# An encoder block on one core: where the values take their tokens' scale, and when late sums and late weights are prepared

## The chip, the cores and the metric

One Trainium2 chip, one of its cores. The metric is the time of one execution in microseconds (us) on the device. TensorE (PE in the profile) multiplies matrices into PSUM; VectorE (DVE), ScalarE (ACT) and GpSimd (POOL) work on whole tiles of 128 partitions; SyncE (SP) starts transfers. Each engine takes its instructions strictly in the order in which they were written for it.

## The reference, cut to what matters

One layer of a hybrid encoder on 256 tokens of width 2048. The mixing half (attention heads and Fourier groups) is left out here. The change lies in the feed-forward half:

```python
h  = rmsnorm(x, norm2_g)                      # per token: x * rstd * g
up = h @ w_up;  gate, val = up[:, :5504], up[:, 5504:]
gate = conv3_over_tokens(gate, dw_w) + dw_b   # depthwise, three neighbouring tokens
act  = gelu(gate) * val
x    = x + act @ w_down
y    = rmsnorm(x, normf_g)
```

The token scale `rstd` of the first norm is one number per token. It must be in the gates before the convolution, which mixes neighbouring tokens, and before the GELU. The value enters as a plain factor of its token's row of `act`, so its scale may be applied anywhere up to the addition to `x`.

## The kernel before

All matmuls are made of three: each operand is split into a high part (a rounded copy, made on ACT) and a low part (the rest, made on DVE as `raw - hi`), and high times high, low times high and high times low are summed in PSUM. So every weight tile of 128x2048 must be loaded (SP), copied (ACT, line 182 or 942) and subtracted (DVE, line 183 or 943) before TensorE can use it. The split tiles (`parts`) have three buffers, the loaded tiles (`raw`) three, and the tiles of the down-projection (`rawd`) two. `PLACES` says at which offset within its buffer a split tile starts: `"moving"` (0, 0), `"thirds"` (0, 32), `"product"` (28, 28) columns for the two parts.

The feed-forward half is a list of items (`ff_items`), one after the other on TensorE: a `gate` or `val` item makes 128 columns of the up-projection for all tokens, transposed (48 matmuls, line 351, or line 338 and 340 for the first ones); a `product` item is one of seven products (`P1`, `P2`, `N3`, `N4`, `N5`, `P6`, `P7`) by which a set of the down-projection over two blocks of tokens and two halves of columns is done with seven block products in place of eight (12 matmuls, lines 1050 to 1052). The sets are (group g, columns c); the last ones are (4, 0) and (4, 1). Four `down` items (24 matmuls each, lines 321 to 323, written as `ps_l`, from `w_down_late`) and four `last` ones (from `w_down_last`, lines 1197 to 1199, written as `ps_e`) do the last seven tiles of the hidden width without the seven products. The order of the items is written out by hand in `PATTERNS`; the end of it is val, down 0, P6, down 1, P2, down 2, N4, down 3 and then the `last` products.

What goes along with item n is set by `ff_step(n)`, called behind the matmuls of item n. It first runs the list `beside[n]`, then splits the weights for item n + 2 (`split_item`, which also starts further loads), then runs the list `behind[n]`. `at(list, n, f, ...)` enters work in these lists. So the place in a list is the place in the queues of ACT and DVE, in front of or after a split that TensorE will need two items later.

- `scaled_sum` (lines 832 to 842) takes a gate or a value out of PSUM at item n + 1 and multiplies it by `r2b`, the tokens' scale spread over all partitions, on DVE. For early items, which leave two sums in PSUM, ACT copies one of them first. `gate_conv`, `gate_gelu` and `val_mult` follow at n + 2.
- `product_out` (1016) adds P2, N3 and N4 to `x` and collects P6 and P7 in `Z`, `down_out` (1054) adds the `down` items' sums to `x`, `last_post` (1072) those of the `last` ones, all on DVE.
- `shared_out` (1029) runs once for each c, at its last set: P1, N5, P6 and P7, which were held over all sets, are combined and added to `x`, in three steps of two, three and three DVE instructions. The steps run behind items n + 2, n + 3 and n + 4, where n is the item P6.
- The weights of `last` 0 to 2 are split as those of other items. `split_last(3)` splits those of `last` 3 into two `rawd` tiles. It is written ahead of `last_product(0, 0)`, the first of the products of `last`. `last_product(c, b)` multiplies by the weights c for the token block b, and then runs `last_post` (addition on DVE, sum of squares on ACT) and `gain` (POOL). The first call also runs the `ff_step` that splits the weights of `last` 2. Then come the final norm's scale (`most_of`, `last_scale`) and `finish`, once for each token block.

Of the kernel before, what the change touches and what calls it, by code (L numbers as in the profile page):

```python
# [9 lines left out]
F32R = mybir.dt.float32r  # L10
AF = mybir.ActivationFunctionType
ALU = mybir.AluOpType

P = 128
D = 2048
S = 256
# [40 lines left out]
LAST = list(range(40, NF))  # L57
# [36 lines left out]
def block_kernel(  # L94
# [18 lines left out]
    nc = tc.nc  # L113
# [14 lines left out]
    units = [(w_in[i], 2048, "first" if i < N_QK else "still") for i in range(24)]  # L128
# [4 lines left out]
    for n, it in enumerate(items):  # L133
        if it[0] == "product":
            continue
        up_index[n] = len(units)
        if it[0] in ("gate", "val"):
            form = "still" if n < FIRST_PRODUCT else "thirds"
            units.append((w_up[2 * it[1] + (it[0] == "val")], 2048, form))
        elif it[0] == "down":  # L140
            units.append((w_down_late[4 * it[1] + it[2]], 2048, "moving"))
        else:
            units.append((w_down_last[it[1]], 512 * len(LAST), "moving"))
    RAW = 3
    raws, halves = {}, {}


    PLACES = {"still": (0, 16), "thirds": (0, 32), "first": (16, 16), "moving": (0, 0), "product": (28, 28)}
# [55 lines left out]
    xs = [base.tile([P, 2, 512], F32, tag=f"xs{c}", name=f"xs{c}") for c in range(4)]  # L204
# [60 lines left out]
    ps = bank(dn, "ps_warm")  # L265
# [13 lines left out]
    def rstd_of(ssq, width, name, n=2, r=None):  # L279

        var = base.tile([P, n], F32, tag="var" + name, name="var" + name)
        nc.vector.tensor_scalar(var, ssq, 1.0 / width, EPS, ALU.mult, ALU.add)
        if r is None:
            r = base.tile([P, n], F32, tag="rstd" + name, name="rstd" + name)
        nc.gpsimd.tensor_tensor(r, var, half_pow[:, 0:n], ALU.pow)
        return r
# [23 lines left out]
    def spread(r, dst, name):  # L310

        nc.vector.tensor_copy(dst, spread_sums(spread_diagonals(r, name), name)[:, :S])
# [76 lines left out]
    for c in range(4):  # L389
        t = base.tile([P, 4, 512], F32R, tag=f"hT{c}", name=f"hT{c}")  # L390
        hT.append(t)
    ps_u = [bank(mm, f"ps_u{b}") for b in range(2)]
    for k in range(NK):
        c, q = k // 4, k % 4
# [4 lines left out]
        hi, lo = halves[c]  # L399
# [392 lines left out]
    for n, (c, kq) in enumerate(OUT_ORDER):  # L792
        i = N_OUT + n
# [14 lines left out]
        if kq >= 2:  # L808
            part = "a" if kq == 2 else "f"
            ps = ps_a[c] if kq < 3 else ps_a[c, "f"]  # L810
# [15 lines left out]
    fp = ctx.enter_context(tc.tile_pool(name="fp", bufs=2))  # L826
# [3 lines left out]
    gate_out, sums_of, act = {}, {}, {}  # L830

    def scaled_sum(ps, name, whole):
        add = fp.tile([P, S], F32, tag="fadd", name=f"fa_{name}", bufs=3)
        if whole:
            nc.vector.tensor_tensor(add, ps[:, 0:S], r2b, ALU.mult)
            sums_of[name] = add
            return
        tmp = fp.tile([P, 512], F32, tag="ftmp", name=f"ft_{name}", bufs=1)[:, 0:S]
        nc.scalar.activation(tmp, ps[:, S : 2 * S], AF.Copy)
        nc.vector.tensor_tensor(add, ps[:, 0:S], tmp, ALU.add)  # L840
        nc.vector.tensor_tensor(add, add, r2b, ALU.mult)
        sums_of[name] = add

    def gate_conv(j):
        ga = sums_of.pop(f"g{j}")
# [170 lines left out]
    def product_out(g, c, p, ps):  # L1016
        tt = nc.vector.tensor_tensor
        if p in ("P6", "P7"):
            z = Z[c, p]
            if g == 0:  # L1020
                nc.scalar.activation(z, ps, AF.Copy)
            else:
                tt(z, ps, z, ALU.add)
        else:
            n, t = {"P2": (0, 0), "N3": (1, 0), "N4": (0, 1)}[p]
            xb = xs[2 * n + c][:, t, :]
            tt(xb, ps, xb, ALU.add)

    def shared_out(c):
        p1, n5, u, p7 = held[c, "P1"], held[c, "N5"], Z[c, "P6"], Z[c, "P7"]  # L1030
        x00, x10, x01, x11 = (xs[2 * n + c][:, t, :] for n in range(2) for t in range(2))
        w = wp.tile([P, 512], F32, tag="junk", name=f"sum01_{c}")
        tt = nc.vector.tensor_tensor
        tt(u, p1, u, ALU.add)
        tt(x00, p1, x00, ALU.add)
        yield
        tt(w, n5, u, ALU.subtract)
        tt(u, u, p7, ALU.add)
        tt(x01, x01, w, ALU.add)
        yield  # L1040
        tt(w, w, p7, ALU.subtract)
        tt(x10, x10, u, ALU.add)
        tt(x11, x11, w, ALU.add)

    def by_parts(ps, o, hi, lo, first, last, tiles, step, at):

# [6 lines left out]

    def down_out(c, pss):
        for b in range(2):
            xb = xs[c][:, b, :]
            nc.vector.tensor_tensor(xb, pss[b], xb, ALU.add)

    ssq3 = base.tile([P, 2, 5], F32, tag="ssq3", name="ssq3")

# [10 lines left out]

    def last_post(c, b, ps, o=0, n=512, part=None):

        xb = xs[c][:, b, o : o + n]
        nc.vector.tensor_tensor(xb, ps, xb, ALU.add)
        square_sum(c, b, c if part is None else part, o, n)

    def most_of(b, n):
# [42 lines left out]
        still_weights(hi, lo, ps, range(12, NK))  # L1121
    tot2 = base.tile([P, 2], F32, tag="tot2", name="tot2")
    nc.vector.tensor_reduce(tot2, ssq2, mybir.AxisListType.X, ALU.add)
    spread(rstd_of(tot2, D, "2"), r2b, "2")
    ff_step(1)
    up_posts(1, *items[0], pair[0][0])
    up_posts(2, *items[1], pair[1][0])
# [1 line left out]
    for n, it in enumerate(items):  # L1129
        if n < 2:  # L1130
            continue
        if it[0] == "last":
            break
        if n in (FIRST_PRODUCT - 9, FIRST_PRODUCT - 8):
            ring_load()
        if n == FIRST_PRODUCT - 6:
            pending.append(lambda: first_sums(*SETS[0]))
        if it[0] in ("gate", "val"):
            kind, j = it
            ps = bank(mm, f"ps_{kind}{j}")  # L1140
            if n < FIRST_PRODUCT:
                still_weights(*halves.pop(up_index[n]), ps, range(NK), lag=4 if n == 2 else 0)
            else:
                still_thirds(*halves.pop(up_index[n]), ps)
            ff_step(n)
            up_posts(n, kind, j, ps)
            continue
        if it[0] == "product":
            kind, g, c, p = it
            hi, lo = halves.pop(it)  # L1150
            both = c == 2
            shape = (2, 1024) if both else (4, 512)
            for cc in (0, 1) if both else (c,):
                o = 512 * cc if both else 0
                if (cc, p) in held:
                    first, end = (g, c) == FIRST_SET[cc], (g, c) == LAST_SET[cc]
                    by_parts(held[cc, p], parts[p], hi, lo, first, end, *shape, o)
                    continue
                ps = bank(mm, f"ps_{p}{g}{cc}")
                by_parts(ps, parts[p], hi, lo, True, True, *shape, o)  # L1160
                at(beside, n + 1, product_out, g, cc, p, ps)
            if (g, c) == LAST_SET.get(c) and p == "P6":
                todo = shared_out(c)
                for m in range(2, 5):
                    at(behind, n + m, next, todo, None)
        else:
            kind, g, c = it
            hi, lo = halves.pop(up_index[n])
            ps = [bank(mm, f"ps_l{g}{c}{b}") for b in range(2)]
            for b in range(2):  # L1170
                moving_weights(hi, lo, 512, LATE, act.get, b, ps[b], True, True)
            at(beside, n + 1, down_out, c, ps)
            if (g, c) == (0, 0):
                gfb = base.tile([P, D], F32, tag="hT0", name="gfb")
                nc.gpsimd.dma_start(gfb, normf_g.partition_broadcast(P))
        ff_step(n)
# [4 lines left out]

    def split_last(c):
        raw, n = raws[i + c], 512 * len(LAST)
        hi = fp.tile([P, 2048], F32R, tag="rawd", name=f"hi{i + c}")
        lo = fp.tile([P, 2048], F32R, tag="rawd", name=f"lo{i + c}")
        halves[i + c] = (hi, lo)
        nc.scalar.activation(hi[:, 0:n], raw[:, 0:n], AF.Copy)
        nc.vector.tensor_tensor(lo[:, 0:n], raw[:, 0:n], f32(hi[:, 0:n]), ALU.subtract)

    def last_product(c, b, o=0, n=512, part=None):  # L1190
        hi, lo = halves[i + c]
        ps = bank(dn, f"ps_e{c}{b}{o}")[:, 0:n]
        for q, k in enumerate(LAST):
            w = slice(q * 512 + o, q * 512 + o + n)
            ah, al = (act[k][:, p * S + b * P : p * S + (b + 1) * P] for p in range(2))
            end = q == len(LAST) - 1
            nc.tensor.matmul(ps, ah, hi[:, w], start=q == 0, stop=False)
            nc.tensor.matmul(ps, al, hi[:, w], start=False, stop=False)
            nc.tensor.matmul(ps, ah, lo[:, w], start=False, stop=end)
        if (c, b) == (0, 0):  # L1200
            ff_step(items.index(("last", 0)))
        last_post(c, b, ps, o, n, part)
        if c < 3:
            gain(c, b)

    split_last(3)
    for c in range(4):
        last_product(c, 0)
    r3 = last_scale(0, 3, most_of(0, 3))
    last_product(0, 1)  # L1210
# [115 lines left out]
```

## Time and profile before

| what | value |
|---|---|
| runs | 958.85, 958.19, 958.24 us, median 958.24 |
| profiled execution | 958.71 us, its span 956.9 us |
| busy, share of the span | PE 98%, DVE 76%, ACT 55%, POOL 5% |
| mean granted TensorE clock | 0.994 |
| HBM read, over the span | 211.80 MB, 224 GB/s |

The span runs from the first to the last instruction of the profiled execution. The 1.8 us between it and that execution's time lie outside of what the profile shows. Times inside the trace are counted from the start of the span.

### The profile page before, as it was taken

Reading aid. Unit: us, or ns where it says so; the run is one execution under the profiler, and the core shown is the slowest. Engines: PE = TensorE matmul, PEld = TensorE weight load, DVE = VectorE, ACT = ScalarE, POOL = GpSimd, SP = SyncE. Lnnn points to the kernel's source line nnn. Section 1 sums busy time; section 2 is a strip of 40 time slices with the busy share of each in tenths; the row PEclk is TensorE's granted clock in tenths of the full one; section 3 lists DMA queues with packets and bytes.
Section 4 is the critical chain, followed back from the end, with each engine's and each line's share of the span. In section 5 each row is a group of like instructions: output and inputs, shape, how many; then the busy total and the mean of one; then the engine's idle time right before and its main releaser. Section 6 shows DMA issues by size and latency. Waiting matters only on the chain.

```text
span 956.9 us, 15064 instructions
## 1 busy us (share of the span) xinstructions
PE 942.1 (98%) x6277; PEld 860.8 (90%) x6277; DVE 725.6 (76%) x862; ACT 525.7 (55%) x585; POOL 47.1 (5%) x62
## 2 busy tenths in 40 slices
PE   9999999999999999999999999999999999999995
PEld 7789999888888999999999999999999999998874
DVE  5668877666578867868877887878978688887784
ACT  5847666544464645456454565555555555555443
POOL 0000000000000000000000000000000000000003
PEclk9999999999999999999999999999999999999998
DMA  8855444455558677677798778887787877878622
GB/s 316 342 180 173 161 148 156 153 176 187 198 217 278 220 237 247 176 258 230 225 297 260 237 226 291 224 256 238 258 268 254 264 226 259 242 230 277 207 101 88
DMA packets 33989, 214.88 MB, mean 225 GB/s; under 512 B 3840, under 2 KB 4352, under 8 KB 9472
## 3 DMA queue, kind: packets, MB, share of 16 engines
q1 hardware_dynamic: 29744, 184.54, 53.0%
q0 software_dynamic: 4032, 29.36, 16.1%
q8 instruction: 49, 0.80, 0.3%
q14 instruction: 20, 0.16, 0.1%
q10 hardware_dynamic: 144, 0.01, 0.0%
HBM read 211.80 MB, written 2.10 MB: 224 GB/s over the span
## 4 chain that ended last, share of the span: by engine, by line
PE 92%; DVE 4%; DMA 2%; ACT 1%; issue 1%; SPq 0%; POOL 0%; ACTq 0%; POOLq 0%; DVEq 0%
PE ps_val L351 21%; PE ps_gate L351 21%; PE ps_q L338 5%; PE ps_P L1051 3%; PE ps_P L1050 3%; PE ps_P L1052 3%; PE ps_N L1050 2%; PE ps_N L1051 2%; PE ps_N L1052 2%; PE ps_q L340 2%; PE ps_a L323 2%; PE ps_a L321 2%; PE ps_a L322 2%; PE ps_gate L338 2%; PE ps_val L338 2%; DMA raw<-in_w_in 2%
## 5 line engine op out<-in xcount | busy, mean ns | idle before, releaser
L183 DVE TENSOR_TENSOR parts<-raw,parts 128x2048 fp32r<-128x2048 f32 (+3 forms) x141 | 303.8, 2155 | 66.4 <-ACT parts L182 66.0
L182 ACT ACTIVATE parts<-raw 128x2048 fp32r<-128x2048 f32 (+3 forms) x140 | 254.6, 1818 | 129.4 <-issue 27.2
L351 PEld LDWEIGHTS ps_val<-hU,parts 128*128 128x128 f32 x1824 | 211.6, 188 | 2.2
L351 PE MATMUL ps_val<-hU,parts 128*128 128x256 f32 x1824 | 212.9, 276 | 0.0
L351 PEld LDWEIGHTS ps_gate<-hU,parts 128*128 128x128 f32 x1776 | 208.3, 189 | 4.6 <-DVE parts L183 2.1
L351 PE MATMUL ps_gate<-hU,parts 128*128 128x256 f32 x1776 | 209.3, 277 | 1.9 <-DVE parts L183 1.9
L338 PE MATMUL ps_q<-hT,parts 128*128 128x512 f32 x192 | 61.3, 393 | 0.0
L1051 PE MATMUL ps_P<-parts_P,op_P 128*128 128x512 f32 x144 | 56.1, 389 | 0.0
L1050 PE MATMUL ps_P<-parts_P,op_P 128*128 128x512 f32 x144 | 56.0, 389 | 0.0
L1052 PE MATMUL ps_P<-parts_P,op_P 128*128 128x512 f32 x144 | 56.0, 389 | 0.0
L943 DVE TENSOR_TENSOR parts_N<-sumw,parts_N 128x2048 fp32r<-128x2048 f32 x18 | 41.2, 2288 | 16.8 <-ACT parts_N L942 16.8
L942 ACT ACTIVATE parts_N<-sumw 128x2048 fp32r<-128x2048 f32 x18 | 34.5, 1916 | 34.6 <-PE ps_val L351 20.0
L340 PE MATMUL ps_q<-hT,parts 128*128 128x256 f32 x192 | 45.5, 278 | 0.0
L1051 PE MATMUL ps_N<-parts_N,op_N 128*128 128x512 f32 x108 | 42.1, 390 | 0.0
L1050 PE MATMUL ps_N<-parts_N,op_N 128*128 128x512 f32 x108 | 42.0, 389 | 0.0
L1052 PE MATMUL ps_N<-parts_N,op_N 128*128 128x512 f32 x108 | 42.0, 389 | 0.0
L338 PEld LDWEIGHTS ps_q<-hT,parts 128*128 128x128 f32 x192 | 35.2, 188 | 6.8
L321 PE MATMUL ps_a<-parts,cat 128*128 128x512 f32 x96 | 37.9, 394 | 0.0
L323 PE MATMUL ps_a<-parts,cat 128*128 128x512 f32 x96 | 37.5, 390 | 0.0
L322 PE MATMUL ps_a<-parts,cat 128*128 128x512 f32 x96 | 37.4, 389 | 0.0
L340 PEld LDWEIGHTS ps_q<-hT,parts 128*128 128x128 f32 x192 | 33.5, 188 | 1.0
L338 PE MATMUL ps_gate<-hU,parts 128*128 128x512 f32 x96 | 32.7, 390 | 0.0
(348 smaller groups left out, 1496.9 us busy)
## 6 DMA issues: line engine op xcount, KB each, us to landing
raw<-in_w_up SPq DMA_DIRECT2D x86, 1024.0 KB, 5.6
raw<-in_w_in SPq DMA_DIRECT2D x21, 1024.0 KB, 4.9
sumw<-in_w_down POOLq DMA_DIRECT2D x18, 1024.0 KB, 8.5
raw<-in_w_out SPq DMA_DIRECT2D x16, 1024.0 KB, 4.8
raw<-in_w_down_late SPq DMA_DIRECT2D x4, 1024.0 KB, 5.1
raw<-in_w_down_last SPq DMA_DIRECT2D x4, 768.0 KB, 4.4
raw<-in_w_in SPq DMA_DIRECT2D x8, 256.0 KB, 6.3
xs<-in_x SPq DMA_DIRECT2D x4, 512.0 KB, 10.6
```

The lines of the kernel that those rows point to most:

```text
L182: nc.scalar.activation(hi[:, s], raw[:, s], AF.Copy)
L183: nc.vector.tensor_tensor(lo[:, s], raw[:, s], f32(hi[:, s]), ALU.subtract)
L321: nc.tensor.matmul(ps, ah, wh, start=first and q == q0, stop=False)
L322: nc.tensor.matmul(ps, al, wh, start=False, stop=False)
L323: nc.tensor.matmul(ps, ah, wl, start=False, stop=last and q == q0 + len(kk) - 1)
L338: nc.tensor.matmul(ps, hi[:, s], h, start=k == 0, stop=False)
L340: nc.tensor.matmul(ps[:, 0:S], lo[:, s], h[:, 0:S], start=False, stop=k == NK - 1)
L351: nc.tensor.matmul(ps[:, 0:S], w[:, s], h[:, o : o + S], start=k == 0 and n == 0, stop=k == NK - 1 and n == 2,)
L943: nc.vector.tensor_tensor(lo, src, f32(hi), ALU.subtract)
L1050: nc.tensor.matmul(ps, o[:, 0, p, :], hi[:, s], start=first and p == 0, stop=False)
L1051: nc.tensor.matmul(ps, o[:, 1, p, :], hi[:, s], start=False, stop=False)
L1052: nc.tensor.matmul(ps, o[:, 0, p, :], lo[:, s], start=False, stop=end)
```

## The change

Values are no longer scaled: where one sum lies in PSUM, ACT copies it; where there are two, they are added and the multiplication is left out. In their place every addition to `x` multiplies by the scale of its token block, by `scalar_tensor_tensor` on DVE in place of `tensor_tensor`. The steps of `shared_out` run behind items n + 1, n + 3 and n + 5. The late weights (`down`, `last`) are split at the offsets of the products. `split_last(3)` stands after `last_product(0, 0)`.

```diff
-            units.append((w_down_late[4 * it[1] + it[2]], 2048, "moving"))
+            units.append((w_down_late[4 * it[1] + it[2]], 2048, "product"))
         else:
-            units.append((w_down_last[it[1]], 512 * len(LAST), "moving"))
+            units.append((w_down_last[it[1]], 512 * len(LAST), "product"))
...
     def scaled_sum(ps, name, whole):
+
         add = fp.tile([P, S], F32, tag="fadd", name=f"fa_{name}", bufs=3)
+        sums_of[name] = add
+        gate = name[0] == "g"
         if whole:
-            nc.vector.tensor_tensor(add, ps[:, 0:S], r2b, ALU.mult)
-            sums_of[name] = add
+            if gate:
+                nc.vector.tensor_tensor(add, ps[:, 0:S], r2b, ALU.mult)
+            else:
+                nc.scalar.activation(add, ps[:, 0:S], AF.Copy)
             return
         tmp = fp.tile([P, 512], F32, tag="ftmp", name=f"ft_{name}", bufs=1)[:, 0:S]
         nc.scalar.activation(tmp, ps[:, S : 2 * S], AF.Copy)
         nc.vector.tensor_tensor(add, ps[:, 0:S], tmp, ALU.add)
-        nc.vector.tensor_tensor(add, add, r2b, ALU.mult)
-        sums_of[name] = add
+        if gate:
+            nc.vector.tensor_tensor(add, add, r2b, ALU.mult)
+
+    def add_scaled(xb, u, b):
+        nc.vector.scalar_tensor_tensor(xb, u, r2[:, b : b + 1], xb, ALU.mult, ALU.add)
...
             n, t = {"P2": (0, 0), "N3": (1, 0), "N4": (0, 1)}[p]
-            xb = xs[2 * n + c][:, t, :]
-            tt(xb, ps, xb, ALU.add)
+            add_scaled(xs[2 * n + c][:, t, :], ps, t)
...
         tt(u, p1, u, ALU.add)
-        tt(x00, p1, x00, ALU.add)
+        add_scaled(x00, p1, 0)
         yield
         tt(w, n5, u, ALU.subtract)
         tt(u, u, p7, ALU.add)
-        tt(x01, x01, w, ALU.add)
+        add_scaled(x01, w, 0)
         yield
         tt(w, w, p7, ALU.subtract)
-        tt(x10, x10, u, ALU.add)
-        tt(x11, x11, w, ALU.add)
+        add_scaled(x10, u, 1)
+        add_scaled(x11, w, 1)
...
         for b in range(2):
-            xb = xs[c][:, b, :]
-            nc.vector.tensor_tensor(xb, pss[b], xb, ALU.add)
+            add_scaled(xs[c][:, b, :], pss[b], b)
...
-        xb = xs[c][:, b, o : o + n]
-        nc.vector.tensor_tensor(xb, ps, xb, ALU.add)
+        add_scaled(xs[c][:, b, o : o + n], ps, b)
...
-    spread(rstd_of(tot2, D, "2"), r2b, "2")
+    r2 = rstd_of(tot2, D, "2")
+    spread(r2, r2b, "2")
...
                 todo = shared_out(c)
-                for m in range(2, 5):
+                for m in (1, 3, 5):
                     at(behind, n + m, next, todo, None)
...
         raw, n = raws[i + c], 512 * len(LAST)
-        hi = fp.tile([P, 2048], F32R, tag="rawd", name=f"hi{i + c}")
-        lo = fp.tile([P, 2048], F32R, tag="rawd", name=f"lo{i + c}")
-        halves[i + c] = (hi, lo)
+        o = PLACES["product"][0]
+        hi, lo = halves[i + c] = [
+            fp.tile([P, 2048], F32R, tag="rawd", name=f"{h}{i + c}")[:, o : o + n]
+            for h in ("hi", "lo")
+        ]
...
+    last_product(0, 0)
     split_last(3)
-    for c in range(4):
+    for c in range(1, 4):
         last_product(c, 0)
```

## The prediction

> **What bounds the kernel now.** I read the page's table of engines first, then who waited for whom on PE, then PE's rows in order of time around the two long waits, the granted clock in short stretches, and last the rows of DVE and ACT in front of those waits.
>
> ```profile
> PE 942.1 (98%) x6277; PEld 860.8 (90%) x6277; DVE 725.6 (76%) x862; ACT 525.7 (55%) x585; POOL 47.1 (5%) x62
> ```
> ```profile
> PE ps_e L1199 <- DVE parts L183: 2.6, 1, 2.6
> PE ps_gate L351 <- DVE parts L183: 1.9, 1, 1.9
> ```
> ```profile
> PE ps_u L321 <- ACT parts L182: 0.9, 1, 0.9
> ```
>
> TensorE is the bound, and it waits in few places. A faster DVE or ACT brings nothing by itself; only what removes one of these waits, or shortens the tail after the last matmul, can. The two longest are both for a low part that DVE made too late (L183), one in the feed-forward half and one at the very end. In order of time (start, duration, what), the first of them:
>
> ```profile
> 830.76 5.44 PE ps_gate L351 x48
> ```
> ```profile
> 863.24 0.39 PE L351 MATMUL ps_gate<-hU,parts 128*128 128x256 f32 x2
> 865.54 7.25 PE L351 MATMUL ps_gate<-hU,parts 128*128 128x256 f32 x46 [1.91 <-DVE parts L183]
> 872.63 0.40 PE L1050 MATMUL ps_N<-parts_N,op_N 128*128 128x512 f32 x1
> ```
>
> A gate's 48 matmuls take 5.44 us. This one began at 863.24 and the next item at 872.63: 9.39 us, so it lost 3.95, twice the 1.91 of the wait. The clock says where the rest went (stretch, length, PE busy, granted clock):
>
> ```profile
> 867.00:868.00 1.00, 1.00 (x7) 0.50 0.68 270
> ...
> 937.00:938.00 1.00, 1.00 (x4) 0.50 0.00 0
> ```
> ```profile
> 12.00:13.00 1.00, 0.09 (x2) 1.00 1.07 412
> ```
>
> Soon after the wait TensorE was granted half its clock. The 46 matmuls took 872.63 - 865.54 = 7.09 us where 46/48 of 5.44 is 5.21: 1.9 us more. The wait at the end is followed by half clock too (937), while the 0.91 us wait near 12 us is not. So a wait of 1.9 us costs about double and one of 0.9 us only itself.
>
> The second place:
>
> ```profile
> 921.91 0.40 PE L321 MATMUL ps_l<-parts,act 128*128 128x512 f32 x1
> 927.17 0.39 PE L323 MATMUL ps_l<-parts,act 128*128 128x512 f32 x1
> 927.40 0.39 PE L1197 MATMUL ps_e<-parts,act 128*128 128x512 f32 x1
> 935.01 0.74 PE L1199 MATMUL ps_e<-parts,act 128*128 128x512 f32 x1 [2.55 <-DVE parts L183]
> 940.38 0.39 PE L1197 MATMUL ps_e<-parts,act 128*128 128x512 f32 x1
> 946.50 0.28 PE L1197 MATMUL ps_e<-hi,act 128*128 128x256 f32 x1
> ```
>
> Between 940.38 and 946.50 are 27 undisturbed matmuls of `last`, 0.227 us each. From 927.40 to 940.38 there are 36, which would take 8.16; they took 12.98, so 4.8 us are lost here. No more than 3.95 + 4.8 = 8.8 us can be won at these two places.
>
> **The spaced steps of `shared_out` and the values' scale, at the first wait.** DVE in order of time, from the split of N4's weights to the split that PE waited for; there is no idle time between these rows:
>
> ```profile
> 846.35 2.29 DVE L943 TENSOR_TENSOR parts_N<-sumw,parts_N 128x2048 fp32r<-128x2048 f32 x1 [1.52 <-ACT parts_N L942]
> 848.55 0.68 DVE L1034 TENSOR_TENSOR z_P<-ps_P,z_P 128x512 f32<-128x512 f32 x1
> 849.15 0.68 DVE L1035 TENSOR_TENSOR xs<-ps_P,xs 128x512 f32<-128x512 f32 x1
> ...
> 859.89 0.68 DVE L1041 TENSOR_TENSOR sum<-sum,z_P 128x512 f32<-128x512 f32 x1
> ...
> 863.20 2.29 DVE L183 TENSOR_TENSOR parts<-raw,parts 128x2048 fp32r<-128x2048 f32 x1
> ```
>
> Each 512-column addition holds DVE for 0.60 us (848.55 to 849.15). The change takes step 1 (two of them) to one item earlier, ahead of 846.35, where DVE sat idle for 1.52 us waiting for ACT; and step 3 (three, from 859.89) to behind the L183 of 863.20. Step 2 stays. That takes 5 x 0.60 = 3.0 us out of the run ahead of that L183.
>
> Against it stand two costs, from these rows (an addition with a scale from a pointer, the same without, and a copy of 256 columns from PSUM by ACT):
>
> ```profile
> L751 DVE SCALAR_TENSOR_TENSOR xs<-ps_a,rstda,xs 128x512 f32<-128x512 f32 x8 | 5.8, 745 | 1.1 <-PE ps_a L323 1.1
> L1027 DVE TENSOR_TENSOR xs<-ps_N,xs 128x512 f32<-128x512 f32 x20 | 13.5, 682 | 0.0
> L1101 DVE SCALAR_TENSOR_TENSOR xs<-xs,rstd,gfb 128x512 f32<-128x512 f32 x2 | 1.5, 746 | 0.0
> L839 ACT ACTIVATE ft_g<-ps_gate 128x256 f32<-128x256 f32 x6 | 2.3, 381 | 13.5 <-PE ps_gate L340 10.8 <-DVE fa_v L840 2.6
> ```
>
> A scaled addition costs 745 - 682 = 63 ns more. Three of them stay in this run (P2, step 2, N4): 0.19 us. The value's copy now stands on ACT ahead of the split that the row of 846.35 waited for, so the run begins up to 0.38 us later. L183 then starts at 863.20 - 3.0 + 0.19 + 0.38 = 860.77 and ends at 863.06. PE wants the low part with its third matmul, at 863.24 + 2 x 0.113 = 863.47. The wait goes, with 0.4 us to spare: 3.95 us won. What is late next: the following split (DVE then does step 3 first, 1.9 us, and its 2.3) ends near 867.2, PE wants it at 863.24 + 5.44 = 868.7. If the cover of 0.4 us is missed, the cost is the miss itself, and only a miss of 1 us and more can bring the clock penalty back.
>
> The Trainium skill (Vector Engine (DVE) Microarchitecture Reference, section Points that are easy to get wrong) says that a scalar-tensor-tensor with two non-bf16 operands in SBUF runs at half throughput. Row L1101 has two such operands and takes 746 ns, as the one with a PSUM operand (745), so the trace does not agree. By the page three additions of steps 2 and 3 would cost 0.6 us more each.
>
> **The values in the rest of the half.** 43 values lose a DVE multiplication, and 38 gain an ACT copy of 0.38 us ahead of a split. The smallest room I found between 330 and 840 us is this one:
>
> ```profile
> 810.93 2.29 DVE L183 TENSOR_TENSOR parts<-raw,parts 128x2048 fp32r<-128x2048 f32 x1
> ```
> ```profile
> 814.28 5.60 PE L351 MATMUL ps_gate<-hU,parts 128*128 128x256 f32 x48
> ```
>
> The split ends at 813.22, PE wants it at 814.28 + 0.23: 1.29 us of room against 0.38. Nothing won, nothing lost: PE hides all of it.
>
> **The end.** Queues of ACT and DVE as they were:
>
> ```profile
> 928.81 1.49 ACT L1187 ACTIVATE hi<-raw 128x1536 fp32r<-128x1536 f32 x1 [5.21 <-DMA raw<-in_w_down_last]
> 930.21 1.47 ACT L182 ACTIVATE parts<-raw 128x1536 fp32r<-128x1536 f32 x1
> 935.59 0.63 ACT L1063 ACTIVATE junkc<-xs 128x512 f32<-128x512 f32 x1 [3.92 <-DVE xs L1075]
> 936.13 0.19 ACT L1063 ACTIVATION_READ_ACCUMULATOR junkc<-xs 128x1 f32 x1
> ```
> ```profile
> 926.70 1.75 DVE L183 TENSOR_TENSOR parts<-raw,parts 128x1536 fp32r<-128x1536 f32 x1
> 930.33 1.76 DVE L1188 TENSOR_TENSOR lo<-raw,hi 128x1536 fp32r<-128x1536 f32 x1 [1.89 <-ACT hi L1187]
> 932.01 1.28 DVE L1057 TENSOR_TENSOR xs<-ps_l,xs 128x512 f32<-128x512 f32 x2
> 933.21 1.75 DVE L183 TENSOR_TENSOR parts<-raw,parts 128x1536 fp32r<-128x1536 f32 x1
> 934.87 1.28 DVE L1075 TENSOR_TENSOR xs<-ps_e,xs 128x512 f32<-128x512 f32 x2
> ```
>
> The split of the last weights (L1187, L1188) waited for its load, and the split of the ones before (L182 at 930.21, L183 at 933.21), wanted first, stood behind it. The change swaps them. I keep this clock (all of it comes 3.95 us earlier after). The ACT part of `last` 2 needs the buffer that `down` 3 frees at 927.17 + 0.39 = 927.56: 927.60 to 929.09. DVE is free by then: its L183 of 926.70 moves up by steps 1 and 3 (3.0 us), down by five scaled additions (0.3), to 924.0; it ends near 925.7, step 3 takes 1.9, the two additions of `down` 3 1.3: 928.9. So the low part of `last` 2 runs 929.13 to 930.88; PE wants it at 927.40 + 20 x 0.227 = 931.9. That wait is gone.
>
> But the last split now stands behind `last_post(0, 0)`, on both queues: the addition 930.79 to 931.54 (0.75), then ACT's square with its read, 0.73 (935.59 to 936.32), to 932.30, ACT's high part to 933.79 (1.49), DVE's low part to 935.59 (1.76), PE at 935.64. Its load is no limit, as it is released by a split that DVE also does earlier. PE wants this low part at 927.40 + 29 x 0.227 = 933.98. A new wait of 1.65 us comes in place of the old ones. After it seven matmuls are left of the 36: the next group starts at 935.64 + 7 x 0.227 = 937.23, plus 0.1 for the restart, where it was 940.38: 3.05 us won, if the clock stays.
>
> Does it stay? About 1.2 us of the 1.65 would show as PE without a matmul, as the first two run meanwhile. It lies between 0.9 (clock kept) and 1.9 (clock halved), nearer to the first. The Trainium skill (TensorE: Matmul & The Clock Gate, section Why this matters for your kernels) has the clock fall only for idle gaps over about 3 us. The trace does not agree, since 1.91 us were enough; by the page the new wait would not cost the clock.
>
> **Small terms.** After the last matmul one addition of the closing chain is a scaled one: +0.06. The late weights at the products' offsets: a `down` item takes 927.40 - 921.91 = 5.49 us where 24 x 0.227 is 5.44. If the place is the reason, some 0.05 for each of four items and the products between can be won, 0.3 in all; if the new place is the worse one, as much is lost. No row shows this place for these tiles; I take 0.1 won, as the regular products run undisturbed there.
>
> **Sum.** 3.95 + 3.05 + 0.1 - 0.06 = 7.0 us. The profiled execution took 958.71, so 951.7 for it. It stands 0.5 above the median, 958.24, for which I say 951.2.
>
> **Rivals.**
> - *The new wait halves the clock.* For it: 1.65 us of lost time is closer to the first wait's than to 0.9 if one counts all of it. Price 7.09 - 5.21 = 1.9 at most, 1.7 at the second place (16 matmuls from 935.01 to 940.38, 5.37 for 3.63): 952.9.
> - *The first wait stays*, because the 0.4 us are used up by something not shown. Then up to 3.95 us are not won: 955.1 at most.
> - *Scaled additions with two SBUF operands cost double.* Two of them, 0.6 each, stand in step 3 ahead of `last` 2, so 1.2 us are added to the new wait and the clock falls: 951.2 + 1.2 + 1.7 = 954.1. Row L1101 speaks against it.
> - *The new wait doesn't come*: the last split is fast enough, another 1.7 won: 949.5.
> - *Slower.* ACT's copies of the values delay each split, and PE waits each time. It would decide from 1.3 us of delay per item. If it did, 38 x 0.38 = 14.4 us would be paid against 7.0 won: 965.6. Room of 1.29 us at the tightest place speaks against it.
> - *Nothing of it holds*: the swap trades one wait for another with half clock, and the first wait stays: within 2 us of now.
>
> **How the numbers follow.** Forecast 0.50; clock halved 0.27; first wait stays 0.08; double cost 0.02; no new wait 0.04; slower 0.05; nothing 0.04. Forecast and halved clock hold 0.77; the range takes in the no-wait case below and the first wait above, with the unknown 0.3: 949.4 to 955.1. About 0.2%, 1.9 us, can be told from no change. Faster 0.91, same 0.04, slower 0.05.
>
> **What would show it.** After: no wait of `ps_gate` L351 near 863; every gate and value at 5.44 us; half clock at most once, near 932 us; one wait of a `ps_e` row for DVE's `lo` of the last split (L1188's successor), about 1.2 us. Wrong if a `ps_gate` wait is still there, if `ps_e` still waits for `parts`, if values wait on ACT in the long stage, or if a scaled addition takes over 0.8 us.

## The result and the profile after

| | before | after |
|---|---|---|
| median of the executions | 958.22 us (957.18 to 958.85, 4) | 951.63 us (951.08 to 952.64, 4) |
| profiled execution, its span | 958.71 us, 956.9 us | 951.68 us, 949.9 us |
| mean granted clock in it | 0.994 | 0.998 |

The ratio is 0.9934, 95% interval 0.9916 to 0.9951: 0.7% faster. PE's longest waits in the profile after (tile and line, what it waited for, us in total, times, longest):

```profile
PE ps_u L321 <- ACT parts L182: 1.1, 2, 0.7
PE ps_e L1207 <- DVE lo L1196: 1.1, 1, 1.1
PE ps_warm L267 <- POOL ones L259: 1.0, 1, 1.0
PE ps_u L323 <- DVE parts L183: 0.5, 1, 0.5
```

The wait of `ps_gate` is gone, and that of `ps_e` is now for `lo`, the last split, no longer for `parts`. The first place, PE and then DVE in order of time (start, duration, what):

```profile
863.68 5.60 PE L351 MATMUL ps_gate<-hU,parts 128*128 128x256 f32 x48
869.12 0.39 PE L1057 MATMUL ps_N<-parts_N,op_N 128*128 128x512 f32 x1
```
```profile
844.60 0.68 DVE L1041 TENSOR_TENSOR z_P<-ps_P,z_P 128x512 f32<-128x512 f32 x1
845.20 0.74 DVE L850 SCALAR_TENSOR_TENSOR xs<-ps_P,rstd,xs 128x512 f32<-128x512 f32 x1
847.06 2.29 DVE L951 TENSOR_TENSOR parts_N<-sumw,parts_N 128x2048 fp32r<-128x2048 f32 x1 [1.12 <-ACT parts_N L950]
...
861.10 2.28 DVE L183 TENSOR_TENSOR parts<-raw,parts 128x2048 fp32r<-128x2048 f32 x1
863.30 0.69 DVE L1048 TENSOR_TENSOR sum<-sum,z_P 128x512 f32<-128x512 f32 x1
```

Step 1 (844.60 and 845.20) now stands in DVE's idle time ahead of 847.06, of which 1.12 us are left; step 3 (L1048) begins behind the L183 that PE needs. That split ends at 863.38, PE wants it with its third matmul at 863.91, and the 48 matmuls take 869.12 - 863.68 = 5.44 us in place of 9.39. The end, in order PE, DVE and ACT:

```profile
918.08 0.39 PE L321 MATMUL ps_l<-parts,act 128*128 128x512 f32 x1
...
923.52 0.39 PE L1205 MATMUL ps_e<-parts,act 128*128 128x512 f32 x1
...
929.85 0.50 PE L1205 MATMUL ps_e<-hi,act 128*128 128x512 f32 x1
930.18 0.39 PE L1206 MATMUL ps_e<-hi,act 128*128 128x512 f32 x1
931.64 0.50 PE L1207 MATMUL ps_e<-lo,act 128*128 128x512 f32 x1 [1.07 <-DVE lo L1196]
...
939.46 0.28 PE L1205 MATMUL ps_e<-hi,act 128*128 128x256 f32 x1
```
```profile
925.24 1.76 DVE L183 TENSOR_TENSOR parts<-raw,parts 128x1536 fp32r<-128x1536 f32 x1
926.91 0.75 DVE L850 SCALAR_TENSOR_TENSOR xs<-ps_e,rstd,xs 128x512 f32<-128x512 f32 x1
929.83 1.76 DVE L1196 TENSOR_TENSOR lo<-raw,hi 128x1536 fp32r<-128x1536 f32 x1 [2.17 <-ACT hi L1195]
```
```profile
927.69 0.63 ACT L1069 ACTIVATE junkc<-xs 128x512 f32<-128x512 f32 x1 [2.49 <-DVE xs L850]
928.23 0.19 ACT L1069 ACTIVATION_READ_ACCUMULATOR junkc<-xs 128x1 f32 x1
928.32 1.47 ACT L1195 ACTIVATE hi<-raw 128x1536 fp32r<-128x1536 f32 x1
```

The chain of the prediction is there link by link: the low part of `last` 2 (925.24), the addition (926.91), the square (927.69), ACT's high part (928.32), DVE's low part (929.83), PE (931.64). From 923.52 to 939.46 are 63 matmuls of 0.227 us, 14.28 us in all; they took 15.94, so 1.66 us are lost here. Before, 946.50 - 927.40 - 14.28 = 4.82 us were lost. The clock stays at full behind this wait (the granted clock is the last column but two):

```profile
932.00:933.00 1.00, 1.00 (x6) 0.84 (x5) 0.91 (x2) 0.66 (x2) 0.00 (x0) 1.00 0.00 0
```

The two spans differ by 7.0 us, and the rows account for it: -3.95 at the first place, -3.16 at the end, -0.37 in the items of the late weights and just behind the first wait, and +0.45 because the second `gate` began at 273.31 in place of 272.86, after longer waits for the first split weights (1.60 us in place of 1.15 in the first 26 us). From the last 18 matmuls on nothing changes: they take 0.06 us less, the closing chain behind them 0.07 more. The waits at the start differ from one profile to another without any change there, by more than 1 us in some of the profiles below.

### The profile page after: what moved, and what is told of

The parts are those of the page before. It is cut to its first block, busy times and chain, and to the rows that moved or that the text cites. A ratio compares the mean times of both kernels' runs of the same rounds, so it can differ in the third digit from the quotient of the medians.

```text
span 949.9 us, 15032 instructions
## 1 busy us (share of the span) xinstructions
PE 937.8 (99%) x6277; PEld 856.6 (90%) x6277; DVE 711.7 (75%) x819; ACT 536.4 (56%) x623; POOL 47.2 (5%) x62
## 4 chain that ended last, share of the span: by engine, by line
PE 95%; DMA 2%; ACT 1%; DVE 1%; issue 0%; POOL 0%; SPq 0%; ACTq 0%; POOLq 0%
PE ps_val L351 22%; PE ps_gate L351 21%; PE ps_q L338 5%; PE ps_P L1059 3%; PE ps_P L1058 3%; PE ps_P L1057 3%; PE ps_N L1059 3%; PE ps_N L1058 3%; PE ps_N L1057 3%; PE ps_q L340 2%; PE ps_a L323 2%; PE ps_a L321 2%; PE ps_a L322 2%; PE ps_gate L338 2%; DMA raw<-in_w_in 2%; PE ps_val L338 2%
## 5 line engine op out<-in xcount | busy, mean ns | idle before, releaser
L183 DVE TENSOR_TENSOR parts<-raw,parts 128x2048 fp32r<-128x2048 f32 (+3 forms) x141 | 303.9, 2155 | 77.9 <-ACT parts L182 77.7
L841 ACT ACTIVATE fa_v<-ps_val 128x256 f32<-128x256 f32 x38 | 14.6, 384 | 88.3 <-PE ps_val L351 88.2
```

What stands on the lines that cost most here:

```text
L183: nc.vector.tensor_tensor(lo[:, s], raw[:, s], f32(hi[:, s]), ALU.subtract)
```

## The experiments

Each experiment starts from the kernel before or from the kernel after, as said. All times are medians of the executions. They were measured in three series, and each ratio is to the kernel before of the same series, which gave 957.26, 957.06 and 957.36 us. The kernel after was not measured again in them; its 951.63 us stand beside the 958.22 above, with the ratio 0.9934.

**One part alone, on the kernel before.** Only the steps' places:

```diff
-                for m in range(2, 5):
+                for m in (1, 3, 5):
```

> The kernel before with the steps of shared_out behind n + 1, n + 3 and n + 5, nothing else. Theory (the steps' places decide both ends): the wait of ps_gate near 863 goes, 3.95 us. At the end DVE is 3 us earlier at the split of last 0, so the load of last 3 starts about 1.2 us earlier too, and the split of last 2, still behind that of last 3, ends near 933.6 in place of 934.96 on the clock of before; wanted at 931.9, a wait of about 1.7 us stays of 2.55. With the clock kept 951.3, with the clock halved 953.0. Rival (each part brings its own share: spacing the first wait, the order of the splits the second): only 3.95 us, 954.3, with the wait of ps_e for parts at 2.5 us and half clock as before.

951.50 us, ratio 0.9936 (0.9919 to 0.9952; the brackets are 95% intervals throughout): as fast as the whole change.

```profile
PE ps_e L1199 <- DVE parts L183: 1.5, 1, 1.5
```

The first wait is gone. The second is still for `parts`, since `last_product(0, 0)` still stands behind the last split, but it is down from 2.55 to 1.46 us, with full clock behind it, and 1.76 us are lost at the end in place of 4.82. The theory holds, the rival falls: moving the steps also frees DVE ahead of the end.

Only the order of the last two splits:

```diff
-    split_last(3)
-    for c in range(4):
+    last_product(0, 0)
+    split_last(3)
+    for c in range(1, 4):
         last_product(c, 0)
```

> The kernel before with split_last(3) behind last_product(0, 0), nothing else. Theory: the first wait stays as it is, 3.95 us with half clock. At the end DVE is late by steps 1 and 3, the low part of last 2 ends near 931.3 on the clock of before (wanted 931.9), the one of last 3 near 936.05 (wanted 933.98): a wait of 2.1 us and half clock, 3.9 us lost in place of 4.8. So 0.9 us faster than before, 957.3. Rival (the order alone removes the second wait as in the changed kernel): 3.05 us faster, 955.2, clock kept.

955.05 us, ratio 0.9978 (0.9968 to 0.9989). The late moments are those of the theory: 2.05 us are lost at the end (PE waits 0.42 for the high and 1.06 for the low part of `last` 3). The time is 2.2 us under its forecast and near the rival's number, but for another reason: the first wait is still there, and no half clock followed either wait in the profiled execution. The same first wait as before, two rows:

```profile
865.45 5.73 PE L351 MATMUL ps_gate<-hU,parts 128*128 128x256 f32 x46 [1.92 <-DVE parts L183]
871.02 0.40 PE L1050 MATMUL ps_N<-parts_N,op_N 128*128 128x512 f32 x1
```

After 1.92 us of waiting 46 matmuls took 5.57 us. After 1.91 us they had taken 7.09 in the profile of before. So the length of the wait alone doesn't decide on the clock.

**One part taken back, from the kernel after.** The steps' old places for c = 0 alone (the second run has `c == 0` in this line, and so the old places for c = 1 alone):

```diff
-                for m in (1, 3, 5):
+                for m in (1, 3, 5) if c == 1 else (2, 3, 4):
```

> The changed kernel with the old places (n + 2, n + 3, n + 4) of the steps for c = 0 alone, those ahead of the first wait. Theory: DVE has steps 1 and 3 (0.60 + 0.66 and 0.60 + 0.66 + 0.66 us) ahead of the split again, which then ends near 866.6, wanted at 863.91 on the changed kernel's clock: a wait of 2.7 us recorded as about 2.5, and 1.9 us of half clock: 951.6 + 4.6 = 956.2. That is more than the 3.95 us of before, as three scaled additions and the values' copy came into the same queue. Rival (the values' relief of DVE carries the gain, the places do not matter): no wait near 863, 951.6.

953.50 us, ratio 0.9958 (0.9944 to 0.9972).

```profile
862.33 0.39 PE L351 MATMUL ps_gate<-hU,parts 128*128 128x256 f32 x2
865.27 5.50 PE L351 MATMUL ps_gate<-hU,parts 128*128 128x256 f32 x46 [2.55 <-DVE parts L183]
870.60 0.39 PE L1057 MATMUL ps_N<-parts_N,op_N 128*128 128x512 f32 x1
```

The wait is back at the forecast length. The item takes 8.27 us, 2.83 too many, and that is the wait with the restart behind it. The time is 2.7 us under its forecast. The forecast's 1.9 us of half clock did not come in the profile, where the waits of the start were 1.3 us shorter too than in the profile after. The rival (no wait) falls.

> The changed kernel with the old places of the steps for c = 1 alone, those ahead of the end. Theory: steps 1 and 3 (3.2 us) stand ahead of the splits of last 0 and last 1, the additions of down 3 end near 926.3, the low part of last 2 near 928.1 (wanted 928.05), the one of last 3 near 932.9 (wanted 930.1): the wait of ps_e grows from 1.07 to about 2.2 us recorded, and the clock is halved behind it: 951.6 + 1.1 + 1.7 = 954.4. If a wait of 2.2 us keeps the clock: 952.7. Rival (only the order of the two last splits matters at the end): 951.6, wait unchanged.

With the old places for c = 1 alone: 953.13 us, ratio 0.9957 (0.994 to 0.9974), between the two numbers of the theory.

```profile
PE ps_e L1207 <- DVE lo L1196: 1.1, 1, 1.1
PE ps_e L1205 <- ACT hi L1195: 0.9, 1, 0.9
```
```profile
934.00:935.00 1.00, 1.00 (x3) 0.50 0.00 0
```

The last split is later on both queues. PE waits for its high part too, 2.0 us in all, and in the profile the clock was halved behind it. The rival (wait unchanged) falls. So the steps' places work at both ends of the sum: those of c = 0 at the first wait, those of c = 1 at the second.

The order of the last splits taken back:

```diff
-    last_product(0, 0)
-    split_last(3)
-    for c in range(1, 4):
+    split_last(3)
+    for c in range(4):
         last_product(c, 0)
```

> The changed kernel with split_last(3) back ahead of last_product(0, 0). Theory (the steps' places had already taken most of the second wait; the order of the splits adds little): the load of last 3 lands 4.4 us after the split of last 0 ends near 919.5, so near 923.9; its two parts run before those of last 2, whose low part ends near 930.2, wanted at 928.06. A wait of about 2.1 us for parts (about 1.5 recorded, as where only the steps were moved) in place of 1.65: 952.0 with the clock kept, 953.7 in executions in which it is halved. Rival (the order takes the second wait): the old loss of 4.8 us returns in place of 1.75, 954.7.

952.15 us, ratio 0.9946 (0.9928 to 0.9965).

```profile
PE ps_e L1207 <- DVE parts L183: 2.0, 1, 2.0
```

The wait for `parts` is 2.02 us where about 1.5 was said, and 2.48 us are lost at the end in place of the 1.66 of the kernel after. The rival (4.8 us lost again) falls. So beside the steps' new places the order is worth 0.8 us by the rows of one profile. The medians differ by 0.5 us, which is within what these times tell apart.

The scale back on the values (those that are added from two sums are multiplied again too):

```diff
-            if gate:
-                nc.vector.tensor_tensor(add, ps[:, 0:S], r2b, ALU.mult)
-            else:
-                nc.scalar.activation(add, ps[:, 0:S], AF.Copy)
+            nc.vector.tensor_tensor(add, ps[:, 0:S], r2b, ALU.mult)
...
-        nc.vector.scalar_tensor_tensor(xb, u, r2[:, b : b + 1], xb, ALU.mult, ALU.add)
+        nc.vector.tensor_tensor(xb, u, xb, ALU.add)
```

> The changed kernel with the tokens' scale back on the values (DVE) and plain additions to x. Theory: nothing on the path hangs on it. Ahead of the first place DVE has three additions of 0.06 us less and starts 0.28 us earlier, so the split near 863 ends about 0.5 us earlier, with no wait either way; at the end the chain to the last split is 0.06 us shorter: 951.5, no difference that can be told. Rival (the relief of DVE by 43 multiplications is what removes the waits): a wait of ps_gate near 863 or a longer one of ps_e, over 953.

951.13 us, ratio 0.9935 (0.9918 to 0.9953). There is no wait of `ps_gate`, and at the end the same 1.1 us as with the change:

```profile
PE ps_e L1203 <- DVE lo L1192: 1.1, 1, 1.1
```

Moving the scale brings nothing that can be measured.

The late weights at the old offsets:

```diff
-            units.append((w_down_late[4 * it[1] + it[2]], 2048, "product"))
+            units.append((w_down_late[4 * it[1] + it[2]], 2048, "moving"))
...
-            units.append((w_down_last[it[1]], 512 * len(LAST), "product"))
+            units.append((w_down_last[it[1]], 512 * len(LAST), "moving"))
...
-        o = PLACES["product"][0]
+        o = PLACES["moving"][0]
```

> The changed kernel with the late weights split at the old offsets (0, 0). Theory: the down items take 5.46 to 5.49 us again and the products between them 2.76 in place of 5.44 and 2.72, 0.3 us in all: 951.9, to be seen in the rows and not in the times. If the offsets are not the reason, the rows stay at 5.44 and 2.72.

951.75 us, ratio 0.9941 (0.9921 to 0.9962), which can't be told from the change. The rows tell it:

```profile
893.38 0.39 PE L321 MATMUL ps_l<-parts,act 128*128 128x512 f32 x1
898.85 0.39 PE L1057 MATMUL ps_P<-parts_P,op_P 128*128 128x512 f32 x1
901.61 0.40 PE L321 MATMUL ps_l<-parts,act 128*128 128x512 f32 x1
```

5.47 us for a `down` item and 2.76 for the product behind it, in place of 5.44 and 2.72. Over the seven items the old offsets cost 0.3 us.

**The wait that was left.** The last split directly behind that of `last` 2, ahead of the addition and the square:

```diff
         if (c, b) == (0, 0):
             ff_step(items.index(("last", 0)))
+            split_last(3)
         last_post(c, b, ps, o, n, part)
...
-    last_product(0, 0)
-    split_last(3)
-    for c in range(1, 4):
+    for c in range(4):
         last_product(c, 0)
```

> The changed kernel with split_last(3) directly behind the split of last 2, ahead of last_post(0, 0). Theory: ACT's high part of last 3 then follows that of last 2 without the addition and the square between, 925.2 to 926.7 (its load lands near 923.9), DVE's low part follows that of last 2, 926.9 to 928.6, wanted at 930.1. No wait of ps_e is left, 1.65 us less: 949.9. last_post(0, 0) comes 1.7 us later, which nobody waits for. Rival (another wait takes its place, such as the load of last 3 or the final scale of block 0): 951 or more.

949.13 us (949.00 to 949.86), ratio 0.9915 (0.9898 to 0.9932): the fastest version here, 2.0 us under the best of the other three of its series. By the rows 1.66 us were to be won.

```profile
923.39 0.39 PE L1205 MATMUL ps_e<-parts,act 128*128 128x512 f32 x1
...
937.67 0.28 PE L1205 MATMUL ps_e<-hi,act 128*128 128x256 f32 x1
```

The 63 matmuls take 14.28 us, with nothing lost. Behind the start PE waits nowhere. The theory holds, the rival falls.

**When the clock falls.** In this last kernel one wait of chosen length was made, by additions on DVE whose result is not used, ahead of the last low part. ("The page's rule" in the expectations is the one of about 3 us that the prediction tells.)

```diff
+        fill = wp.tile([P, 512], F32, tag="junk", name="fill")
+        for _ in range(5):                      # 5, 6, 7, 8
+            nc.vector.tensor_tensor(fill, gfb[:, 0:512], gfb[:, 512:1024], ALU.add)
```

> The kernel with the last split directly behind that of last 2, and five more additions of 512 columns on DVE (result unused, 0.60 us each) ahead of the low part of last 3, which then comes 1.6 us late (928.5 + 3.0 against 930.0). Asked is what share of the executions gets half clock behind a wait of this length. Theory A (the wait's length decides): none, as behind the 0.9 us near 12 us; all at 950.7. Theory B (the clock is judged in stretches of 3.4 us whose place against the program changes from one execution to the next, and falls if TensorE did less than about half of one): none or few; 950.7. The page's rule, about 3 us of idle: none.

> As with five, with six additions: late by 2.2 us, 951.3 with full clock, 953.0 with half. Theory A: as the wait of 1.9 us was followed by half clock in the profile of before, all executions have it. Theory B: about 6 in 10. The page's rule: none.

> As before, with seven additions: late by 2.8 us, 951.9 with full clock, 953.6 with half. Theory A: all. Theory B: about 8 in 10. The page's rule: none.

> As before, with eight additions: late by 3.4 us, 952.5 with full clock, 954.2 with half. Theory A: all. Theory B: nearly all (97 in 100). The page's rule: it sets in here, all or most.

| additions | median us | wait in the profile, us | clock behind it in the profile | executions with a mean clock of 0.995 or less |
|---|---|---|---|---|
| 5 | 953.00 | 1.97 | half | 4 of 6 |
| 6 | 953.43 | 2.70 | full | 2 of 6 |
| 7 | 954.90 | 3.42 | full | 7 of 12 |
| 8 | 955.79 | 4.15 | half | 8 of 12 |

The low parts came later than said, since an addition held DVE for 0.70 us here and not for 0.60 (why is not shown). With five of them, start and duration:

```profile
926.94 3.59 DVE L1197 TENSOR_TENSOR fill<-gfb 128x512 f32<-128x512 f32 x5
930.44 1.75 DVE L1199 TENSOR_TENSOR lo<-raw,hi 128x1536 fp32r<-128x1536 f32 x1
```

So the medians lie 0.4 to 2.3 us above the nearer number of each forecast, and with five additions the low part is 2.1 us late in the profile, near what was meant for six. So the half clock in at least four of its six executions is no test of the theories' "none" or "few". The counts are lower bounds: the mean clock is given to 0.001, and the execution above with 3.4 us of half clock (old places for c = 1) had a mean of 0.997. From the profiles, one row of the granted clock (last column but two) behind the wait of 1.97 us, one behind that of 4.15 us, and the wait of 3.42 us with a row of the clock behind it:

```profile
934.00:935.00 1.00, 1.00 (x3) 0.50 0.00 0
```
```profile
936.00:937.00 1.00, 1.00 (x4) 0.50 0.00 0
```
```profile
PE ps_e L1210 <- DVE lo L1199: 3.4, 1, 3.4
```
```profile
934.00:935.00 1.00, 1.00 (x6) 1.00 0.00 0
```

Theory A falls: 1.97 us were followed by half clock and 3.42 us were not. The rule of the Trainium skill (TensorE: Matmul & The Clock Gate, section Why this matters for your kernels), a fall only for idle gaps over about 3 us, does not agree with the same two rows. The shares of theory B are neither shown nor excluded by the counts: at least 2 of 6 and 8 of 12 are seen where it had 6 in 10 and nearly all.

The rest of theory B is borne out by the traces. In each of the 14 profiles the granted clock changes only at whole multiples of 3.41 us from its other changes (in that of the kernel before at 866.8, 870.2, 935.1, 938.5 and 952.2 us), and the place of this grid, counted from the start of the span, differs by up to 2 us between the profiles. Cut along its grid, a profile shows what decides. These are the stretches around the two waits of the kernel before, and those that share the wait of 3.42 us (stretch, length, PE busy, clock in the stretch):

```profile
863.42:866.83 3.41, 1.50 (x12) 1.00 0.84 276
931.68:935.10 3.42, 0.82 (x3) 1.00 0.00 0
```
```profile
927.91:931.32 3.41, 1.69 (x8) 1.00 0.00 0
931.32:934.74 3.42, 1.72 (x8) 1.00 0.00 0
```

| profile | waits, us | PE busy in the stretches that hold them, of 3.41 us | clock in the next stretch |
|---|---|---|---|
| before, first and second place | 1.91; 2.55 | 1.50; 0.82 | half; half |
| old places for c = 1 | 0.91 and 1.07 | 1.52 | half |
| 5 additions | 1.97 | 1.44 | half |
| 8 additions | 4.15 | 1.45 and 1.21 | half, half |
| 7 additions | 3.42 | 1.69 and 1.72 | full, full |
| 6 additions | 2.70 | 2.03 and 2.09 | full, full |
| old places for c = 0 | 2.55 | 2.34 and 1.92 | full, full |
| order alone, first place | 1.92 | 2.34 and 2.57 | full, full |
| order taken back | 2.02 | 2.59 and 2.21 | full, full |

In all 14 profiles, from the first full clock on, half clock follows each stretch in which PE was busy for up to 1.52 us, and full clock each one in which it was busy for longer (the highest of the first kind and the lowest of the second both read 1.52). So a wait of 3.42 us that the grid cuts in two nearly equal parts keeps the clock, and a wait of 1.91 us that falls into one stretch loses it. This was read from the traces afterwards; PE's busy time rests on modelled ends of matmuls, and no run was made to test the border. What sets the place of the grid is open, so one profile can't tell whether another execution pays for a wait.

## Why the prediction was right

The number was 951.2, the measured one 951.63, and the likeliest case came about, with its working at both waits. Its rule for the clock was wrong.

- *First wait.* Forecast: split ends 0.4 us ahead of PE, 3.95 us won. Measured: 863.38 against 863.91, 0.5 us ahead, 9.39 to 5.44. The ledger of additions moved out, scaled additions, and the delay by the copy held to about a tenth of a microsecond.
- *End.* Forecast: the last split 1.65 us late, about 1.2 of it seen as a wait, 1.75 lost with the restart. Measured: 1.54 late (931.64 against 923.52 + 29 x 0.227 = 930.10), 1.07 seen, 1.66 lost. Won there: 3.16 against 3.05.
- *Clock.* This step was wrong in its kind, though not in its outcome here. I read "a wait of 1.9 us costs about double" from two waits that were both followed by half clock. The runs show the same wait of 1.9 us without it, and waits of 2.55 and 3.42 us as well; what counts is how much of one stretch of the grid a wait takes. That the new wait of 1.07 us kept the clock fits both readings: PE was busy for 2.29 us of its stretch (929.24 to 932.65).
- *Luck.* The forecast counts both prices of half clock in the kernel before as won in full. They come in some executions only: of 23 executions of the kernel before in the last series, 7 had a mean clock of 0.994 or less (957.7 to 959.85 us), as in the profile with two half-clocked stretches, and 2 had 0.998 (954.86 and 955.46). That the executions counted from (median 958.24) lay near that profile is luck; the later series have medians about 1 us lower. So some 3.5 of the 6.6 us (955.2 - 951.6, from two executions of another series) are the waits and the offsets, which come in every execution. By rows they are 2.1 + 1.4 + 0.3, with the half clock's 1.9 and 1.7 us taken off at the two places. The rest is half clock, which the kernel before mostly had once or twice and the changed one was not seen to have.
- *Late weights.* Mis-sized: 0.1 taken, 0.3 measured, at the end of the bounds that were given. The rows of the experiment with the old offsets show that the place is the reason.
- *Values.* Forecast: nothing won, nothing lost. Measured: all gates and values between 330 us and the end take 5.44 us, and the kernel takes 951.13 with the scale on the values. The scaled additions cost 744 to 745 ns, from PSUM and from SBUF alike:

```profile
L850 DVE SCALAR_TENSOR_TENSOR xs<-ps_N,rstd,xs 128x512 f32<-128x512 f32 x20 | 14.7, 745 | 0.0
L850 DVE SCALAR_TENSOR_TENSOR xs<-sum,rstd,xs 128x512 f32<-128x512 f32 x4 | 3.0, 744 | 0.0
```

  So the rival with the double cost falls. The sentence of the Trainium skill about it (Vector Engine (DVE) Microarchitecture Reference, section Points that are easy to get wrong: half throughput with two non-bf16 sources in SBUF) does not agree with the second row, 744 ns.
- *What was not seen beforehand.* I gave the spacing the first wait and, in the sum, the order of the splits the second, although the working for the end has the steps' 3.0 us in it. The spacing alone does nearly all of both: with it alone 1.76 us are lost at the end, with the whole change 1.66.

## What to carry to other kernels

When PE is the bound, list its few waits. For each, write the ledger of the queue in front of the late instruction: what can go to an idle stretch earlier, what can go behind it. Where two chains are swapped, follow the one that is now last link by link: an addition and a square in front of the last split cost 1.66 us that a one-line move gave back. A wait of TensorE of about 2 us and more has a second price, half clock for 3.4 us, that comes in some executions and not in others. Don't size it from one profile.

## What the runs showed of the hardware

- Half clock came with recorded waits of 1.91, 1.97, 2.55 and 4.15 us in one profiled execution each, and did not come with waits of 1.92, 2.02, 2.55, 2.70 and 3.42 us in others. At the first place the 46 matmuls took 7.09 us with it (behind 1.91 us of waiting, kernel before) and 5.57 without (behind 1.92, order alone).
- In the 14 profiles the clock changes on a grid of 3.41 us whose place differs by up to 2 us between them. Half clock followed a stretch in which PE was busy for up to 1.52 us, full clock one in which it was busy for longer.
- Where split weights lie in their buffer changes TensorE's rate a little: 5.46 to 5.49 us for 24 matmuls at offsets (0, 0), 5.44 at (28, 28), while the next weights are being split. Why is not shown.
